# Sample-convolution products, the gated block's low part and a fill on GpSimd instead of VectorE, in layer 0's first channel mixer

## The chip, the cores and the metric

The kernel runs on one core of a Trainium2 chip. The core has five engines that run side by side, each through its own queue in program order: PE (TensorE, matmuls and transposes), DVE (VectorE), ACT (ScalarE), POOL (GpSimd) and SP (SyncE, which issues nearly all DMAs here). An instruction starts when those ahead of it on its engine are done and when the semaphores it waits for have been raised. The metric is the device time of one execution in microseconds, as the median of the runs.

## The reference

One inference step of a decoder trunk with two layers, width 1024, in fp32, for a prompt of 1024 positions and for 8 samples of 8 new positions each (64 more columns, 1088 in all). What matters here is layer 0:

```
glu = a_val * sigmoid(a_gate)                  # 512 channels
ext = concat([conv_prev, glu], axis=1)         # sample: 30 stored rows + 8 new ones
a   = causal_depthwise_conv(ext, conv_w) + b   # 31 taps for each channel
a   = silu(layer_norm(a))
b   = stick_breaking_attention(q, k, v, ...)   # samples: 8 pages of 128 keys each
h   = h + concat([a, b]) @ w_out
h   = h + (silu(g) * u) @ w_ffn_out            # g, u = split(rms_norm(h) @ w_ffn_in), 2816 each
```

For a sample the convolution of one channel is, for each of its 8 new positions, a sum over 31 products of a stored or new row with a tap.

## The kernel before, in words

Activations lie channel by channel: 128 channels on the partitions, positions along the free axis. The positions are worked on in two groups: GA, the first 512 prompt positions, and GB, the other 512 and the 64 sample columns (576). A matrix product is made in three passes from operands that are split into a high part (rounded by ACT to fp32r) and a low part (the exact value less the high part). So each weight tile `hl` costs one ACT copy (L184) and two POOL subtractions of 128x512 (L186), made up to two tiles ahead of the one in use; and each operand costs one ACT copy (L240) and one subtraction (L241), both in the helper `split`.

While PE runs the output projection and the channel mixer of GA in layer 0, the mixing work of GB is threaded in behind it. This is a background flow (`flow_c`): a Python generator that is advanced by one piece at each slot between the mixer's matmul groups. The place of a piece in every engine's queue is fixed by that at build time; nothing is scheduled at run time. The flow is, in order: the attention of GB, then the convolution of GB (`conv_b`) interleaved with the attention of the samples over their cached pages (`sample`), then the layer norm of the convolution (`conv_norm`).

The channel mixer of GA is `run_ffn` with `sig=True`; no other call has it. For each of 22 blocks f: DVE scales the gate's result out of PSUM into a buffer `tmp` (L291), ACT makes the sigmoid (L474), POOL multiplies the two (L475); DVE scales the other half (L291); at the next flush POOL multiplies both (L500, in `gated`); at the flush after that `split` makes the high part on ACT (L240) and the low part (L241) of `hid`. Two blocks later `hid` is multiplied by the second weight and DVE adds the result to the residual (L295). `tmp` has four buffers, taken in turn.

`conv_b` works on four chunks c of 128 channels. For each, DVE adds 31 taps over the 512 prompt positions into a PSUM tile `cacc` (L863, L865), two taps in a piece. After tap 11 PE transposes the stored rows (L888) and ACT copies them behind the prompt's columns in `ext` (L889). After taps 13, 15, 17 and 19 `steps` makes two sample positions each: two products of 128x248 (8 samples by 31 taps, L873) into a `tmp`, and one sum over the taps (L874).

`sample` makes, for each page group, transposes of key pages on PE (L1121), their split by ACT (L1124) and DVE (L1125, and L1132 for the new keys), scores on PE (L1144) and their gathering (L1154 on ACT, L1155 on DVE); for each of four pairs of samples it then makes the weights (L1173, L1179), fills a tile `wx` with zeros (L1181), copies the new keys' weights into it (L1184, ACT), and transposes everything (L1193) for the products with the value pages (L1216).

## Time and profile before

| what | us |
|---|---|
| median of 3 runs | 2554.57 (2547.91 to 2555.24) |
| profiled execution, device time | 2549.7 |
| its span, first to last instruction | 2547.9 |
| DVE busy in the span | 1701.0 (67%) |
| POOL busy in the span | 1566.5 (61%) |
| PE busy in the span | 2434.8 (96%) |

The span is what the trace covers; the device time of that execution is 1.8 us more. Busy times say how long an engine had an instruction running; matmuls overlap in PE's pipeline, so a busy PE is not always a PE at full rate. In the answers of the trace, a row of the windows view gives a stretch (us from the span's start), its length, then for each engine its busy time with the number of instructions, the clock granted to PE, the DMA engines' share and GB/s. A row of the timeline gives start, duration, engine, line, operation and tiles; in brackets stands the idle time of the engine before it and what ended it. A row of a group gives busy us and mean ns of one instruction behind the first bar.

### The profile page before, as it was taken

The numbers are of one execution on the slowest core, as the hardware profiler recorded it, in microseconds if no ns is written. First come the engines' busy times: TensorE is split into PE (matmuls) and PEld (weight loads), VectorE is DVE, ScalarE is ACT, GpSimd is POOL, SyncE is SP. The second block draws the span as 40 slices with busy tenths as digits, with TensorE's granted clock in tenths as the row PEclk, the third lists the DMA queues.
The fourth block names the chain that finished last, engine by engine and source line by source line (L and its number), as shares of the span: only waits on it lengthen the run. The fifth ranks groups of instructions, "written<-read, shape, count | busy, mean of one in ns | idle before, by whom it ended". The sixth has DMA issues, their size and how long they took to land.

```text
span 2547.9 us, 41426 instructions
## 1 busy us (share of the span) xinstructions
PE 2434.8 (96%) x15871; PEld 2194.1 (86%) x15871; DVE 1701.0 (67%) x2359; ACT 1104.0 (43%) x1875; POOL 1566.5 (61%) x1205
## 2 busy tenths in 40 slices
PE   8999989999999899999999999998999999999998
PEld 6789877787777678989999889888888888999997
DVE  3696877977878743766566533448776778666655
ACT  4536867753444343443433421234334334443333
POOL 6754244444443356678877622267888886887775
PEclk9999999999999999999999999999999999999999
DMA  7342241244565435223223311152333332333322
GB/s 222 115 114 74 65 118 38 75 116 122 172 178 156 136 96 159 75 67 100 86 86 94 123 42 43 49 157 59 100 92 93 98 92 84 99 96 104 100 84 79
DMA packets 355485, 258.31 MB, mean 101 GB/s; under 512 B 22913, under 2 KB 303617, under 8 KB 355272
## 3 DMA queue, kind: packets, MB, share of 16 engines
q1 hardware_dynamic: 355256, 255.66, 34.1%
q8 instruction: 126, 2.06, 0.3%
q14 instruction: 71, 0.58, 0.1%
q10 hardware_dynamic: 32, 0.01, 0.0%
HBM read 237.41 MB, written 18.69 MB: 101 GB/s over the span
## 4 chain that ended last, share of the span: by engine, by line
PE 43%; DVE 9%; POOL 3%; issue 2%; ACT 1%; POOLq 0%; DVEq 0%; ACTq 0%
PE acc L235 22%; PE acc L521 19%; DVE sum L200 2%; POOL hl L197 2%; DVE hid L241 1%; DVE hb L295 1%; DVE sum L201 1%; DVE sum L202 1%; DVE tmp L525 0%; DVE b L1677 0%; POOL tmp L500 0%; DVE sum_c L214 0%; DVE fb L1681 0%; DVE x L1677 0%; PE blk L1900 0%
## 5 line engine op out<-in xcount | busy, mean ns | idle before, releaser
L186 POOL TENSOR_TENSOR hl<-stage,hl 128x512 fp32r<-128x512 f32 x464 | 639.5, 1402 | 456.1 <-ACT hl L184 334.9
L235 PE MATMUL acc<-x,hl 128*128 128x512 f32 (+1 forms) x3648 | 781.7, 352 | 13.6 <-ACT hl L184 3.3
L235 PEld LDWEIGHTS acc<-x,hl 128*128 128x128 f32 x3648 | 587.5, 190 | 76.2 <-issue 4.9
L235 PE MATMUL acc<-hid,hl 128*128 128x288 f32 (+1 forms) x3096 | 553.7, 334 | 19.0 <-DVE hb L295 8.8
L235 PEld LDWEIGHTS acc<-hid,hl 128*128 128x128 f32 x3096 | 472.1, 190 | 74.6 <-DVE hb L295 12.6
L295 DVE TENSOR_TENSOR hb<-acc,hb 128x512 f32<-128x512 f32 (+1 forms) x360 | 255.9, 717 | 176.0 <-PE acc L235 174.7
L521 PE MATMUL acc<-x,hl 128*128 128x288 f32 (+1 forms) x2676 | 362.1, 290 | 4.7 <-POOL hl L197 1.9
L521 PEld LDWEIGHTS acc<-x,hl 128*128 128x128 f32 x2676 | 348.9, 188 | 7.0 <-POOL hl L197 2.5
L197 POOL TENSOR_TENSOR hl<-sum,hl 128x512 fp32r<-128x512 f32 x180 | 237.7, 1349 | 174.6 <-ACT hl L196 174.4
L184 ACT ACTIVATE hl<-stage 128x1024 fp32r<-128x1024 f32 x232 | 243.5, 1055 | 224.3 <-PE acc L235 140.3
L525 DVE TENSOR_TENSOR tmp<-acc,tmp 128x288 f32<-128x288 f32 (+1 forms) x420 | 173.3, 441 | 228.3 <-ACT tmp L537 135.5
L197 POOL TENSOR_TENSOR hl<-stage,hl 128x512 fp32r<-128x512 f32 x180 | 266.8, 1504 | 13.0 <-ACT hl L196 13.0
L521 PE MATMUL acc<-b,hl 128*128 128x256 f32 (+1 forms) x1548 | 216.5, 291 | 14.9 <-DVE tmp L525 11.9
L521 PEld LDWEIGHTS acc<-b,hl 128*128 128x128 f32 x1548 | 202.2, 189 | 20.4 <-ACT hl L196 13.6
L235 PE MATMUL acc<-x1t,hl 128*128 128x288 f32 x1152 | 216.3, 296 | 1.5 <-POOL hl L186 1.5
L235 PEld LDWEIGHTS acc<-x1t,hl 128*128 128x128 f32 x1152 | 195.9, 188 | 19.5 <-POOL hl L186 1.7
L196 ACT ACTIVATE hl<-sum 128x512 fp32r<-128x512 f32 x180 | 103.1, 623 | 241.3 <-DVE sum L202 219.9
L291 DVE TENSOR_TENSOR tmp<-acc,rr 128x512 f32<-128x512 f32 (+1 forms) x108 | 75.0, 708 | 106.1 <-PE acc L235 94.0
L500 POOL TENSOR_TENSOR tmp<-tmp 128x576 f32<-128x576 f32 (+1 forms) x85 | 126.3, 1486 | 16.3 <-ACT tmp L477 8.3
L196 ACT ACTIVATE hl<-stage 128x512 fp32r<-128x512 f32 x180 | 105.6, 618 | 67.7 <-PE acc L235 62.4
L241 DVE TENSOR_TENSOR hid<-tmp,hid 128x512 fp32r<-128x512 f32 (+1 forms) x88 | 99.3, 1130 | 46.0 <-ACT hid L240 45.7
L235 PE MATMUL acc<-x1a,hl 128*128 128x512 f32 x480 | 122.4, 408 | 3.0 <-POOL hl L186 1.3
(290 smaller groups left out, 3161.4 us busy)
## 6 DMA issues: line engine op xcount, KB each, us to landing
stage<-in_w_ffn_in_dram SPq DMA_DIRECT2D x176, 512.0 KB
stage<-in_w_ffn_out_dram SPq DMA_DIRECT2D x88, 512.0 KB
stage<-in_w_in_even_dram SPq DMA_DIRECT2D x40, 512.0 KB
kst<-in_cache_k_dram SPq DMA_DIRECT2D x64, 256.0 KB
vst<-in_cache_v_dram SPq DMA_DIRECT2D x64, 256.0 KB
stage<-in_w_out_even_dram SPq DMA_DIRECT2D x16, 512.0 KB
stage<-in_w_in_odd_dram SPq DMA_DIRECT2D x16, 512.0 KB
stage<-in_w_out_odd_dram SPq DMA_DIRECT2D x16, 512.0 KB
```

Of the source, the lines that this page charges most:

```text
L184: act.activation(hl[:, 0], st, AF.Copy)
L186: pool.tensor_tensor(hl[:, 1, c], st[:, c], f32(hl[:, 0, c]), op=OP.subtract)
L196: act.activation(hl[:, 0, c], x, AF.Copy)
L197: pool.tensor_tensor(hl[:, 1, c], x, f32(hl[:, 0, c]), op=OP.subtract)
L200: todo = [lambda: dve.tensor_tensor(sb, su[:, lo], su[:, hi], op=OP.add), lambda: dve.tensor_tensor(sa[:, hi], sg[:, lo], su[:, lo], op=OP ...
L235: pe.matmul(acc[:, b, :c1 - c0], w, xs[:, xi, c0 - o:c1 - o], start=first and s == 0, stop=last and s == 2)
L241: (on or dve).tensor_tensor(dst[:, 1], src, f32(dst[:, 0]), op=OP.subtract)
L291: dve.tensor_tensor(d, a, r, op=OP.mult)
L295: dve.tensor_tensor(d, a, d, op=OP.add)
L500: (dve if both and f == NF - 1 else pool).tensor_tensor(t[:, :n], t[:, :n], u[:, :n], op=OP.mult)
L521: pe.matmul(acc[:, :w2], h[:, wi, i, k], xk[:, xi], start=k == 0 and s == 0, stop=k == 3 and s == 2)
L525: dve.tensor_tensor(out, acc[:, :w2], x, op=OP.add)
```

## The change

Four edits, all in work that stands in layer 0's first channel mixer (the call with `sig=True`) or in `flow_c` behind it:

- In `gated` the low part of `hid` (L241) is made by POOL instead of DVE where `sig` is true: 22 subtractions of 128x512.
- In `steps` the products (L873) are made by POOL: 32 of 128x248.
- The sums over the taps (L874, 16 of them) stay on DVE, but each is issued after the next tap of an even number instead of right behind its products, that is in the flow's next piece.
- The zero fill of `wx` (L1181), four times, is made by POOL.

Behind the added lines the numbers move by up to two: L888 becomes L890, L1121 L1123, L1125 L1127, L1181 L1183.

```diff
             def fin():
                 (dve if both and f == NF - 1 else pool).tensor_tensor(t[:, :n], t[:, :n], u[:, :n], op=OP.mult)
-                late.append(lambda: split(dst, t[:, :n]))
+                late.append(lambda: split(dst, t[:, :n], on=pool if sig else None))
             post.append(fin)
...
                 for q in range(2):
-                    dve.tensor_tensor(p[:, q], es[:, :, q0 + q:q0 + q + CW], taps, op=OP.mult)
-                dve.tensor_reduce(new[:, q0:q0 + 2], p, axis=mybir.AxisListType.X, op=OP.add)
-
-            LATE = 6
+                    pool.tensor_tensor(p[:, q], es[:, :, q0 + q:q0 + q + CW], taps, op=OP.mult)
+                pend.append(lambda: dve.tensor_reduce(new[:, q0:q0 + 2], p, axis=mybir.AxisListType.X, op=OP.add))
+
+            LATE, pend = 6, []
...
                 tap(acc, ext[:, j:j + HALF], j)
                 if j % 2 == 0:
+                    while pend:
+                        pend.pop()()
                     continue
...
-                dve.memset(wx[bp], 0.0)
+                pool.memset(wx[bp], 0.0)
```

How the queues change, at three places. DVE, first chunk, around the third and fourth pair of sample positions (L1125 splits the transposed keys in `kth`, L291 scales a gate out of PSUM). Before:

```order
L865 SCALAR_TENSOR_TENSOR cacc<-ext,par,cacc 128x512 x2
L873 TENSOR_TENSOR tmp<-ext,par 128x248 x2
L874 TENSOR_REDUCE snew<-tmp 128x16
L865 SCALAR_TENSOR_TENSOR cacc<-ext,par,cacc 128x512 x2
L873 TENSOR_TENSOR tmp<-ext,par 128x248 x2
L874 TENSOR_REDUCE snew<-tmp 128x16
L1125 TENSOR_TENSOR kth<-m,kth 128x256 x2
L1132 TENSOR_TENSOR kth<-knew,kth 128x2x8
L241 TENSOR_TENSOR hid<-tmp,hid 128x512
L291 TENSOR_TENSOR tmp<-acc,rr 128x512
```

and after, from the second pair's sum on:

```order
L865 SCALAR_TENSOR_TENSOR cacc<-ext,par,cacc 128x512
L874 TENSOR_REDUCE snew<-tmp 128x16
L865 SCALAR_TENSOR_TENSOR cacc<-ext,par,cacc 128x512 x2
L874 TENSOR_REDUCE snew<-tmp 128x16
L865 SCALAR_TENSOR_TENSOR cacc<-ext,par,cacc 128x512
L1127 TENSOR_TENSOR kth<-m,kth 128x256 x2
L1134 TENSOR_TENSOR kth<-knew,kth 128x2x8
L291 TENSOR_TENSOR tmp<-acc,rr 128x512
L865 SCALAR_TENSOR_TENSOR cacc<-ext,par,cacc 128x512
L874 TENSOR_REDUCE snew<-tmp 128x16
```

The products and the low part of `hid` are gone from the queue, and each sum stands one tap behind where it stood.

POOL at the same chunk, all four pairs (L475 multiplies a gate by its sigmoid, L500 multiplies both halves). Before:

```order
L475 TENSOR_TENSOR tmp<-tmp 128x512
L186 TENSOR_TENSOR hl<-stage,hl 128x512 x4
L500 TENSOR_TENSOR tmp<-tmp 128x512
L475 TENSOR_TENSOR tmp<-tmp 128x512
L186 TENSOR_TENSOR hl<-stage,hl 128x512 x4
L500 TENSOR_TENSOR tmp<-tmp 128x512
```

and after:

```order
L475 TENSOR_TENSOR tmp<-tmp 128x512
L186 TENSOR_TENSOR hl<-stage,hl 128x512 x2
L873 TENSOR_TENSOR tmp<-ext,par 128x248 x2
L186 TENSOR_TENSOR hl<-stage,hl 128x512 x2
L873 TENSOR_TENSOR tmp<-ext,par 128x248 x2
L500 TENSOR_TENSOR tmp<-tmp 128x512
L475 TENSOR_TENSOR tmp<-tmp 128x512
L873 TENSOR_TENSOR tmp<-ext,par 128x248 x2
L186 TENSOR_TENSOR hl<-stage,hl 128x512 x2
L873 TENSOR_TENSOR tmp<-ext,par 128x248 x2
L241 TENSOR_TENSOR hid<-tmp,hid 128x512
L186 TENSOR_TENSOR hl<-stage,hl 128x512 x2
```

The four pairs of products stand between the weight tiles' low parts, the last behind L475, and a low part of `hid` follows them.

POOL a little later, at the first fill of `wx`. Before:

```order
L500 TENSOR_TENSOR tmp<-tmp 128x512
L475 TENSOR_TENSOR tmp<-tmp 128x512
L186 TENSOR_TENSOR hl<-stage,hl 128x512 x4
L500 TENSOR_TENSOR tmp<-tmp 128x512
L186 TENSOR_TENSOR hl<-stage,hl 128x512 x4
```

and after:

```order
L500 TENSOR_TENSOR tmp<-tmp 128x512
L475 TENSOR_TENSOR tmp<-tmp 128x512
L1183 MEMSET wx 128x128
L186 TENSOR_TENSOR hl<-stage,hl 128x512 x2
L241 TENSOR_TENSOR hid<-tmp,hid 128x512
L186 TENSOR_TENSOR hl<-stage,hl 128x512 x2
L500 TENSOR_TENSOR tmp<-tmp 128x512
```

The fill now stands behind a product that waits for ACT's sigmoid.

## The prediction, as it was made before the result was known

> **What bounds the kernel now.** I first read the page's shares of the engines, then the stage that the change touches (430 to 982 us of the span), cut at the places where the products L873 stand. The windows view (busy PE, PEld, DVE, ACT, POOL) of four stretches that hold the products of the four chunks, with their sum, and the sum of the three stretches between them:

> ```profile
> 592.00:616.00 24.00, 20.73 (x97) 16.48 (x95) 22.44 (x35) 7.33 (x15) 12.13 (x9) 0.95 0.40 111
> 671.00:692.00 21.00, 19.16 (x105) 14.86 (x103) 19.13 (x34) 8.13 (x17) 7.08 (x5) 1.00 0.64 195
> 753.00:776.00 23.00, 18.18 (x101) 13.28 (x100) 21.79 (x34) 6.66 (x15) 9.02 (x7) 0.93 0.59 174
> 836.00:858.00 22.00, 19.34 (x111) 14.84 (x104) 19.06 (x32) 7.05 (x16) 8.76 (x6) 0.95 0.58 168
> sum 90.00, PE 77.41 PEld 59.46 DVE 82.42 ACT 29.18 POOL 36.98; mean PE 19.35 PEld 14.87 DVE 20.60 ACT 7.30 POOL 9.25
> ...
> sum 176.00, PE 172.27 PEld 139.81 DVE 138.30 ACT 82.19 POOL 73.16; mean PE 57.42 PEld 46.60 DVE 46.10 ACT 27.40 POOL 24.39
> ```

> Between the product stretches PE is busy 172.27 of 176 us (97.9%) and DVE 79%. In them DVE is busy 82.42 of 90 us (92%) and PE only 77.41 (86%). PE is the engine that sets the end elsewhere; here it waits for DVE, and the granted clock is 0.93 to 0.95 in three of the four. The timeline of PE shows each wait, and that PE runs slower right after the longer ones:

> ```profile
> 577.66 3.04 PE L235 MATMUL acc<-x,hl 128*128 128x512 f32 x12
> 585.38 0.42 PE L888 MATMUL m<-ident,stc 120*128 120x120 f32 x2 [1.90 <-DVE kth L1125]
> 585.56 4.59 PE L235 MATMUL acc<-x,hl 128*128 128x512 f32 x12
> 611.09 0.77 PE L1121 MATMUL m<-ident,kst 128*128 128x128 f32 x4 [2.42 <-DVE kth L1125]
> 612.71 4.70 PE L235 MATMUL acc<-hid,hl 128*128 128x512 f32 x12 [0.84 <-DVE tmp L291]
> 689.64 0.75 PE L1144 MATMUL z<-kth,qb 128*128 128x264 f32 x4 [1.84 <-DVE zs L1155]
> 762.63 1.66 PE L235 MATMUL acc<-hid,hl 128*128 128x512 f32 x6 [1.17 <-DVE tmp L291]
> 766.40 2.34 PE L235 MATMUL acc<-hid,hl 128*128 128x512 f32 x6 [2.11 <-DVE hb L295]
> 769.42 2.08 PE L235 MATMUL acc<-hid,hl 128*128 128x512 f32 x6
> 855.94 1.11 PE L1121 MATMUL m<-ident,kst 128*128 128x128 f32 x4 [2.66 <-DVE kth L1125]
> 856.70 4.22 PE L235 MATMUL acc<-x,hl 128*128 128x512 f32 x12
> ```

> Twelve matmuls take 3.04 us at full rate, but 4.59, 4.70 and 4.22 after waits of 1.90, 2.42 and 2.66; six take 2.34 and 2.08 after 2.11, against 1.66 after a short wait. The wait of 1.84 shows no slow burst behind it. So a wait near 2 us costs itself and about 1.2 to 1.7 more. That DVE is late because of the products, its own timeline shows for the first chunk:

> ```profile
> 604.25 2.39 DVE L873 TENSOR_TENSOR tmp<-ext,par 128x248 f32<-128x248 f32 x2
> 606.67 0.67 DVE L874 TENSOR_REDUCE snew<-tmp 128x16 f32<-128x496 f32 x1
> 607.26 1.53 DVE L865 SCALAR_TENSOR_TENSOR cacc<-ext,par,cacc 128x512 f32<-128x512 f32 x2
> 608.70 1.30 DVE L873 TENSOR_TENSOR tmp<-ext,par 128x248 f32<-128x248 f32 x2
> 610.03 0.67 DVE L874 TENSOR_REDUCE snew<-tmp 128x16 f32<-128x496 f32 x1
> 610.62 0.75 DVE L1125 TENSOR_TENSOR kth<-m,kth 128x256 fp32r<-128x256 f32 x2
> ```

> DVE runs without a gap, and PE's wait at 611.09 ends with the L1125 that stands behind two pairs of products (3.7 us).

> **The change, part by part.** The rows that price it: the products on DVE in the four stretches (first sum) and the low parts L241 there (second), then groups of the trace.

> ```profile
> sum 90.00, DVE 27.42; mean DVE 6.85
> ...
> sum 90.00, DVE 2.74 POOL 0.00; mean DVE 0.68 POOL 0.00
> ...
> 585.84 0.37 ACT L889 ACTIVATE ext<-m 128x240 f32<-128x240 f32 x1 [0.72 <-PE m L888]
> 579.07 0.68 DVE L241 TENSOR_TENSOR hid<-tmp,hid 128x512 fp32r<-128x512 f32 x1
> L873 DVE TENSOR_TENSOR tmp<-ext,par x32: 584/746/1720, 592.2 to 854.3; 128x248 f32<-128x248 f32 x32
> L1125 DVE TENSOR_TENSOR kth<-m,kth 128x256 fp32r<-128x256 f32 x32 | 12.1, 415 | 8.2 <-ACT kth L1124 8.2
> L475 POOL TENSOR_TENSOR tmp<-tmp 128x512 f32<-128x512 f32 x11 | 14.7, 1338 | 52.5 <-ACT tmp L474 49.4 <-PE m L1121 3.1
> L1913 POOL TENSOR_TENSOR ss<-ss,tmp 128x320 f32<-128x320 f32 x6 | 5.2, 867 | 7.3 <-ACT tmp L1909 7.0
> L1913 POOL TENSOR_TENSOR ss<-ss,tmp 128x256 f32<-128x256 f32 x6 | 4.4, 737 | 7.1 <-ACT tmp L1909 7.0
> ```

> *Products leave DVE (the main term).* The four stretches lose 27.42 us of products and 2.74 us of L241; 52.3 us of DVE work stay. If the waits go, PE needs its 77.41 us less the slow bursts (4.70 and 4.22 against 3.04, twice six against 1.66: 1.66 + 1.18 + 1.10 = 3.9 us), so 73.5 us, at the 97.9% of the stretches between: 75.1 us instead of 90. DVE would then be at 70%, below the 79% that goes with hardly any waits. That is 14.9 us at most.

> *Products on POOL.* The trace has no POOL instruction with these operands (a broadcast, and taps that stand four columns apart). Lower bound: 737 ns for 256 columns, with (867 - 737) / 64 = 2.0 ns a column, is 0.72 us for 248. Upper bound: DVE's own longest, 1.72 us. Between them a hint: on DVE the fastest product took 584 ns where 256 columns in one row took 415, 1.41 times as long; at that ratio POOL would take 1.0 us. I take 1.0 us, P from here on.

> [...]

> *Does POOL keep up?* Of the 32 products 30 lie in the stretches. POOL's work there becomes 36.98 + 4 low parts at 1.34 (L475's mean for the same shape) + 30 P = 42.3 + 30 P: 63.9 us at the lower bound, 72.3 at P = 1.0, against 75.1 there are. So POOL fits, at 96%, but it also waits for ACT's copies in its queue, and the sums, now a piece later, wait for POOL. What helps: the first pair of a chunk needs only L889's copy (done at 586.2 us in the first chunk), so it can run before the stretch begins at 592. What hurts: a later pair stands behind L475, which waits for DVE's L291 and ACT's sigmoid. From that L291 to the pair's sum DVE has about 4 us of other work (three taps at 0.77, a sum at 0.67, a key split at 0.75 and L1155), POOL and ACT need about 2 us and 2 P. So DVE waits little at P = 1.0, and 1.4 us a chunk at P = 1.7; behind it stand L1125, L1155 and L295, for which PE waits. At 96% POOL queues will form that this does not count: I take 3 us off the main term, a fifth, 14.9 - 3 = 11.9 us.

> *Weights behind the products.* A pair of products delays the low parts L186 behind it by 2 P = 2 us. Their cover is the distance: `hl` is made two tiles ahead of the one in use, and the 24 matmuls of one tile take 6.1 us by the row above without the flow's work between. Nothing is paid unless POOL falls behind by more than that. Buffers are the other new link: in this stage 23 of DVE's L291 now wait for a POOL instruction on the same `tmp` instead of 8, but nearly all for an L475, L500 or L241 that is queued well ahead.

> *Low parts of hid on POOL, outside the stretches.* Of 22, 18 remain: about 12 us of DVE time in the rest of the stage. One matters: at 579.07 us L241 stood ahead of the L291 whose chain (sigmoid, weight copy, L1154, L1155, the key copies) ends in the 1.90 us wait at 585.38. With 0.68 us less the wait falls to about 1.2, below those that had a slow burst: 0.7 + 1.55 = 2.2 us; or nothing, if another part of the chain holds. I take 1.5. In the attention of GB ahead (430 to 560 us) five fall away from DVE, but POOL's fills of `be` queue behind them:

> ```profile
> 430.00:560.00 130.00, 124.29 (x806) 101.05 (x806) 105.79 (x104) 86.66 (x142) 64.73 (x59) 0.99 0.26 73
> 449.40 0.14 PEld L1014 LDWEIGHTS m<-ident,be 128*128 128x128 f32 x1 [2.25 <-POOL be L992]
> 446.43 1.75 DVE L241 TENSOR_TENSOR hid<-tmp,hid 128x512 fp32r<-128x512 f32 x1
> ```

> PE waits there 5.7 us in all. The wait at 449.40 is for a POOL fill behind four low parts that ran while this L241 did; without it 0 to 3 us are gained, and a low part before a fill costs 0 to 2. I take +0.5. At the stage's end the last L241 no longer stands behind L295 on DVE, but behind two L186 on POOL, and is ready earlier: +0.4.

> *The fill.* It is short on either engine; what counts is its place on POOL:

> ```profile
> 649.37 1.49 POOL L475 TENSOR_TENSOR tmp<-tmp 128x512 f32<-128x512 f32 x1 [3.12 <-PE m L1121]
> 653.38 0.60 ACT L1194 ACTIVATE wts<-m 128x512 f32<-128x512 f32 x1 [1.10 <-PE m L1193]
> ```

> At the first and third pair of samples it stands behind L475, which ended at 650.86 at the first: ACT's copies into `wx` (at 649.9 now) and the key copies behind them come some 1.2 us later, nearly covered by the 1.10 us that ACT waits soon after. Cost 0 to 1; I take 0.3.

> Sum: 11.9 + 1.5 + 0.5 + 0.4 - 0.3 = 14.0 us less. All work behind 982 us is unchanged and follows later PE by PE, so the gain reaches the end. The profiled execution took 2549.7 us (span 2547.9 and 1.8 around it): 2535.7. It lies 4.9 us below the median of the three runs, 2554.57, which gives 2540.6. I forecast **2538 us**, between the two; the rivals start from 2552, likewise.

> **Rivals.** *POOL becomes the bound, slower.* The place is the four stretches: at P = 1.6 their POOL work is 90 us, and the gain is gone; beyond that sums wait for products, L295 and L1125 wait behind the sums, and late weights follow. At P = 2.0 it is 102 us, 12 us more than now: 2564. For it speaks that no row shows POOL with such operands; against it, that P would have to exceed even DVE's longest product, 1.72, which it only took while POOL was running.

> *Nothing that can be measured.* P near 1.5 (87 us of POOL work in 90), or new waits for `tmp` and for value pages eat the gain. For pages it speaks that PE waits for them now, against it that the first of these waits (4.4 us in seven) comes at 883 us, behind the stretches:

> ```profile
> 877.30 1.09 PE L1193 MATMUL m<-ident,bet 128*128 128x128 f32 x8 [1.24 <-DVE bet L1179]
> PE o L1216 <- DMA vst<-in_cache_v_dram: 4.4, 7, 1.3
> 883.85 0.62 PE L1216 MATMUL o<-vst,wts 128*32 128x256 f32 x4 [0.59 <-DMA vst<-in_cache_v_dram]
> ```

> 2549 to 2554.

> *More than the sum.* Sums never wait (3 us), the wait at 449.40 goes with its slow burst (3 us), and the one at 877.30 (1.24 us, for the weights' L1179) too: 14 + 7 = 21 us, 2531 or below.

> **How the numbers follow.** The forecast (2532 to 2546) has 0.55, more than the sum 0.13, nothing measurable 0.22, POOL as the bound 0.10. A measurement of this kernel tells about 0.3% (7.7 us) from no change. So faster 0.68, within 0.3% 0.22, slower 0.10. The range holds the first two cases and most of the third: 2528 to 2554. The likeliest case's own range is 2532 to 2546.

> **What would show it right or wrong.** In the profile after: L873 on POOL at about 1.0 us, in four stretches that together take about 77 us instead of 90; no wait of PE above 1.5 us for DVE there, and no slow burst behind; DVE at 70 to 75%; L874 waiting under 1 us for POOL. It would be wrong if L873 takes 1.5 us or more on POOL, if PE's waits keep their places with POOL as the last releaser, or if the stage as a whole (430 to 982 us) does not become shorter by 10 us.

## The result, and the profile after

The changed kernel takes 2526.09 us (median of 7 runs, 2522.38 to 2535.0), the kernel before 2548.51 us beside it (7 runs, 2542.94 to 2555.24): a ratio of 0.992, 95% interval 0.9906 to 0.9934, or 22.4 us less. The profiled execution took 2532.55 us, 17.2 less than the profiled one of before: its stage, cut below, is 21.8 us shorter, but begins 4.3 us later, ahead of any instruction that was changed. The page's head and its shares of the engines after:

```profile
span 2530.7 us, 41450 instructions
PE 2431.9 (96%) x15871; PEld 2195.4 (87%) x15871; DVE 1659.3 (66%) x2301; ACT 1105.2 (44%) x1875; POOL 1615.9 (64%) x1263
```

DVE lost 42 us of work and POOL got 49 more, while PE's 15871 matmuls stand in the same order in both kernels. So the two traces can be cut at the same matmuls, and each piece compared. The windows view of before and then of after (busy PE, PEld, DVE, ACT, POOL; clock, DMA share, GB/s): the attention of GB, the piece up to the first products, the piece from the last products to the end of the stage; then the sum of the three pieces between the product stretches.

```profile
433.90:560.20 126.30, 120.63 (x791) 98.83 (x790) 104.39 (x97) 86.39 (x141) 64.93 (x59) 0.99 0.27 76
560.20:592.08 31.88, 29.98 (x145) 24.94 (x144) 22.60 (x37) 12.78 (x24) 12.22 (x11) 0.95 0.65 184
858.14:981.93 123.79, 115.32 (x553) 85.39 (x552) 68.43 (x93) 48.92 (x75) 71.37 (x51) 0.98 0.39 117
...
sum 176.19, PE 172.46 PEld 140.00 DVE 138.69 ACT 81.96 POOL 73.38; mean PE 57.49 PEld 46.67 DVE 46.23 ACT 27.32 POOL 24.46
```

```profile
438.22:564.91 126.69, 120.45 (x790) 98.89 (x790) 101.57 (x92) 86.62 (x141) 70.18 (x64) 0.99 0.27 75
564.91:594.99 30.08, 28.43 (x145) 23.82 (x144) 22.02 (x36) 12.79 (x24) 15.98 (x14) 1.00 0.65 192
841.96:964.44 122.48, 113.83 (x554) 84.42 (x552) 64.09 (x85) 48.49 (x75) 77.87 (x57) 1.00 0.39 119
...
sum 175.60, PE 172.23 PEld 139.64 DVE 131.06 ACT 81.10 POOL 86.44; mean PE 57.41 PEld 46.55 DVE 43.69 ACT 27.03 POOL 28.81
```

And the four product stretches, the sum before and all four after:

```profile
sum 89.87, PE 77.28 PEld 59.31 DVE 82.09 ACT 29.41 POOL 36.68; mean PE 19.32 PEld 14.83 DVE 20.52 ACT 7.35 POOL 9.17
```

```profile
594.99:613.96 18.97, 18.97 (x97) 15.99 (x95) 14.74 (x27) 8.21 (x17) 16.32 (x16) 1.00 0.40 120
668.59:687.22 18.63, 18.63 (x105) 14.88 (x103) 14.44 (x25) 8.71 (x17) 11.72 (x11) 1.00 0.68 205
747.64:763.38 15.74, 15.74 (x100) 11.99 (x99) 14.05 (x25) 6.77 (x15) 15.22 (x15) 1.00 0.79 232
823.93:841.96 18.03, 18.03 (x108) 14.25 (x101) 14.50 (x26) 7.43 (x17) 13.75 (x13) 1.00 0.65 182
sum 71.37, PE 71.37 PEld 57.10 DVE 57.72 ACT 31.12 POOL 57.01; mean PE 17.84 PEld 14.28 DVE 14.43 ACT 7.78 POOL 14.25
```

The stage from 433.90 to 981.93 us became 21.8 us shorter: the attention +0.4, the piece before the first products -1.8, the four stretches -18.5, the pieces between them -0.6, the tail -1.3. In the stretches PE is now busy without a gap (71.37 of 71.37 us) at clock 1.00. Of the 18.5 us, 12.6 were idle time of PE (89.87 - 77.28) and 5.9 were matmuls that took longer (77.28 - 71.37). About 4.2 of these 5.9 are the lower clock: the clock of the stretches before was 0.94, 1.00, 0.93 and 0.95, and the missing shares of 24.12, 22.92 and 21.99 us add up to that.

The moved work in the groups of after (minimum, median, maximum in ns; first and last start):

```profile
L873 POOL TENSOR_TENSOR tmp<-ext,par x32: 842/857/896, 590.8 to 835.5; 128x248 f32<-128x248 f32 x32
L241 POOL TENSOR_TENSOR hid<-tmp,hid x22: 1268/1296/2129, 453.3 to 951.1; 128x512 fp32r<-128x512 f32 x22
L874 DVE TENSOR_REDUCE snew<-tmp x16: 655/664/666, 597.7 to 839.5; 128x16 f32<-128x496 f32 x16
```

No sum L874 waits for POOL. A product took 0.857 us, between the prediction's lower bound of 0.72 and the 1.0 that it took for P. PE's timeline after shows what is left of the waits of which the prediction spoke:

```profile
453.38 0.33 PE L1016 MATMUL m<-ident,be 128*128 128x128 f32 x1 [1.68 <-POOL be L994]
589.84 0.42 PE L890 MATMUL m<-ident,stc 120*128 120x120 f32 x2 [1.65 <-DVE kth L1127]
590.02 3.04 PE L235 MATMUL acc<-x,hl 128*128 128x512 f32 x12
860.52 1.09 PE L1195 MATMUL m<-ident,bet 128*128 128x128 f32 x8 [1.24 <-DVE bet L1181]
```

The wait at 585.38 is 0.25 us shorter and, more important, has lost the slow burst behind it (3.04 for 4.59 us): 1.8 us together.

### The profile page after: what moved, and what is told of

Same layout as the page of the kernel before. It is cut to its first block, busy times and chain, and to the rows that moved or that the text cites. A ratio compares the mean times of both kernels' runs of the same rounds, so it can differ in the third digit from the quotient of the medians.

```text
span 2530.7 us, 41450 instructions
## 1 busy us (share of the span) xinstructions
PE 2431.9 (96%) x15871; PEld 2195.4 (87%) x15871; DVE 1659.3 (66%) x2301; ACT 1105.2 (44%) x1875; POOL 1615.9 (64%) x1263
## 4 chain that ended last, share of the span: by engine, by line
PE 43%; DVE 10%; POOL 2%; issue 2%; ACT 1%; POOLq 0%; DVEq 0%; ACTq 0%
PE acc L235 22%; PE acc L521 20%; DVE sum L200 2%; POOL hl L197 2%; DVE hb L295 1%; DVE hid L241 1%; DVE sum L201 1%; DVE sum L202 0%; DVE sum_c L214 0%; DVE b L1679 0%; DVE tmp L525 0%; POOL tmp L500 0%; DVE fb L1683 0%; PE blk L1902 0%; DVE x L1679 0%
## 5 line engine op out<-in xcount | busy, mean ns | idle before, releaser
L186 POOL TENSOR_TENSOR hl<-stage,hl 128x512 fp32r<-128x512 f32 x464 | 634.0, 1390 | 409.2 <-ACT hl L184 296.5
L235 PE MATMUL acc<-x,hl 128*128 128x512 f32 (+1 forms) x3648 | 782.8, 352 | 13.0 <-DVE tmp L291 3.0
L235 PEld LDWEIGHTS acc<-x,hl 128*128 128x128 f32 x3648 | 588.3, 190 | 74.9 <-issue 5.7
L235 PE MATMUL acc<-hid,hl 128*128 128x288 f32 (+1 forms) x3096 | 551.3, 334 | 13.0 <-DVE hb L295 5.5
L235 PEld LDWEIGHTS acc<-hid,hl 128*128 128x128 f32 x3096 | 471.3, 190 | 66.4 <-DVE hb L295 7.9
L295 DVE TENSOR_TENSOR hb<-acc,hb 128x512 f32<-128x512 f32 (+1 forms) x360 | 256.5, 719 | 178.7 <-PE acc L235 177.6
L235 PE MATMUL acc<-x1t,hl 128*128 128x288 f32 x1152 | 216.3, 295 | 1.5 <-POOL hl L186 1.5
L235 PEld LDWEIGHTS acc<-x1t,hl 128*128 128x128 f32 x1152 | 195.9, 188 | 19.5 <-POOL hl L186 1.7
L291 DVE TENSOR_TENSOR tmp<-acc,rr 128x512 f32<-128x512 f32 (+1 forms) x108 | 75.2, 711 | 139.9 <-PE acc L235 123.3
L500 POOL TENSOR_TENSOR tmp<-tmp 128x576 f32<-128x576 f32 (+1 forms) x85 | 124.7, 1468 | 9.2 <-ACT tmp L477 8.2
L235 PE MATMUL acc<-x1a,hl 128*128 128x512 f32 x480 | 122.4, 409 | 2.7 <-POOL hl L186 1.3
L252 POOL TENSOR_TENSOR ss<-ss,tmp 128x512 f32<-128x512 f32 (+1 forms) x69 | 105.1, 1523 | 29.0 <-ACT tmp L251 18.8
```

The costliest lines, as they stand in the source:

```text
L186: pool.tensor_tensor(hl[:, 1, c], st[:, c], f32(hl[:, 0, c]), op=OP.subtract)
L235: pe.matmul(acc[:, b, :c1 - c0], w, xs[:, xi, c0 - o:c1 - o], start=first and s == 0, stop=last and s == 2)
L252: pool.tensor_tensor(ss[:, g.cs], ss[:, g.cs], t[:, :g.n], op=OP.add)
L291: dve.tensor_tensor(d, a, r, op=OP.mult)
L295: dve.tensor_tensor(d, a, d, op=OP.add)
L500: (dve if both and f == NF - 1 else pool).tensor_tensor(t[:, :n], t[:, :n], u[:, :n], op=OP.mult)
```

## The experiments

In all of them the four stretches are cut at the same matmuls as above. The lengths in us, from the windows view of each run (PE's and POOL's share follow where they matter):

| kernel | chunk 1 | 2 | 3 | 4 | sum |
|---|---|---|---|---|---|
| before | 24.12 | 20.84 | 22.92 | 21.99 | 89.87 |
| after | 18.97 | 18.63 | 15.74 | 18.03 | 71.37 |
| products and later sums alone | 18.98 | 18.64 | 15.75 | 18.02 | 71.39 |
| low parts alone | 24.47 | 22.50 | 24.04 | 21.80 | 92.81 |
| half of the products | 19.00 | 18.64 | 19.22 | 18.05 | 74.91 |
| sums at once | 20.38 | 18.63 | 16.98 | 18.05 | 74.04 |
| later sums alone | 23.01 | 19.18 | 20.78 | 19.57 | 82.54 |
| products twice on POOL | 21.04 | 18.64 | 17.64 | 18.02 | 75.34 |
| products on DVE, taps in PSUM | 19.72 | 20.45 | 20.12 | 24.12 | 84.41 |
| more page buffers | 18.98 | 18.64 | 15.74 | 18.02 | 71.38 |

### Products and later sums alone

The changed kernel with the low parts and the fill given back to DVE:

```diff
-                late.append(lambda: split(dst, t[:, :n], on=pool if sig else None))
+                late.append(lambda: split(dst, t[:, :n]))
...
-                pool.memset(wx[bp], 0.0)
+                dve.memset(wx[bp], 0.0)
```

> The products on GpSimd with their sums a piece later, alone; the low parts of hid and the fill of wx stay on VectorE. My theory (VectorE was late because of the products): PE's waits in the four product stretches go as in the changed kernel, which reached the same matmuls 18.5 us earlier there; 18 to 20 us below the kernel before in all, ratio 0.992 to 0.993. Rival A (any VectorE time counts alike: the change took 27.4 us of products and 15 us of low parts off): two thirds of 22 us, so 14 to 15 us, ratio 0.994 to 0.9945.

Measured: 2527.82 us against 2545.35, ratio 0.993 (0.9913 to 0.9946), 17.5 us. The stretches are those of after to a few hundredths of a us. So the main term is this part's alone; what the other parts add can't be told apart in the time. By the traces the stage (433.90 to 981.93 us before) takes 529.6 us here against 526.2 after; of these 3.4 us, 1.8 are the piece before the first products, where the slow burst is still there.

### Low parts alone

The kernel before with one line of the change:

```diff
-                late.append(lambda: split(dst, t[:, :n]))
+                late.append(lambda: split(dst, t[:, :n], on=pool if sig else None))
```

> The low parts of hid on GpSimd, alone; products and fill stay on VectorE. My theory: one low part leaves each stretch (2.7 of 82.4 us of VectorE work), so the waits there become little shorter; with the wait at 585 us some 2 to 5 us gained, ratio 0.998 to 0.9995. Rival A (any VectorE time counts alike): one third of 22 us, 7 to 8 us, ratio 0.997. Rival B (GpSimd's fills and weight parts queue behind the low parts): slower, ratio 1.000 to 1.002.

Measured: 2544.89 us against 2545.35, ratio 0.9996 (0.9986 to 1.0005): nothing that can be told from no change. The trace shows a gain and a loss. The piece ahead of the first products loses its slow burst here too (1.8 us). But the stretches get 2.9 us longer, though 2.7 us of work left DVE there. The group of products on DVE, and PE's first long wait, in this run:

```profile
L873 DVE TENSOR_TENSOR tmp<-ext,par x32: 589/906/1735, 589.9 to 854.5; 128x248 f32<-128x248 f32 x32
```

```profile
609.79 1.09 PE L1121 MATMUL m<-ident,kst 128*128 128x128 f32 x4 [3.55 <-DVE kth L1125]
```

The median product took 906 ns instead of 746, and the wait at L1121 is 3.55 us instead of 2.42. POOL's new work made DVE's products slower: in the stretches they took 31.05 us instead of 27.34, 3.7 more, against the 2.7 that had left.

### Half of the products

As the first experiment, but of each pair one product on POOL and one on DVE:

```diff
-                    pool.tensor_tensor(p[:, q], es[:, :, q0 + q:q0 + q + CW], taps, op=OP.mult)
+                    (pool if q else dve).tensor_tensor(p[:, q], es[:, :, q0 + q:q0 + q + CW], taps, op=OP.mult)
```

> Of each two products one on GpSimd and one on VectorE, sums a piece later, nothing else changed. If what matters is whether VectorE is over some 80% busy in a stretch (79% went with hardly any waits between the stretches): half of the products leave it at about 69 of 76 us or under 90% and the waits mostly go, 13 to 18 us gained, ratio 0.993 to 0.995. If the gain goes with the time taken off: half of what the products bring, 8 to 10 us, ratio 0.996 to 0.997.

Measured: 2528.89 us, ratio 0.9936 (0.9919 to 0.9954), 16.5 us. Three stretches are as short as with all products moved; only the third is not, and its row shows why:

```profile
740.52:759.74 19.22, 17.25 (x101) 12.72 (x99) 18.28 (x31) 6.66 (x15) 11.43 (x10) 0.94 0.76 225
...
757.15 4.60 PE L235 MATMUL acc<-hid,hl 128*128 128x512 f32 x12 [1.97 <-DVE hb L295]
```

One wait of 1.97 us with its slow burst (4.60 for 3.04) makes up the 3.5 us. The sums come later here too, and that alone brings 7.3 us in the stretches (below). On top of it half of the products bring 7.6 us, where all of them bring 11.2. So the gain is not in proportion to the work taken off DVE; it is complete in a stretch once PE's waits there are gone, since PE then has no gap left.

### Sums at once

The changed kernel with each sum right behind its products:

```diff
-                pend.append(lambda: dve.tensor_reduce(new[:, q0:q0 + 2], p, axis=mybir.AxisListType.X, op=OP.add))
+                dve.tensor_reduce(new[:, q0:q0 + 2], p, axis=mybir.AxisListType.X, op=OP.add)
```

> The changed kernel, but each sum issued right behind its products instead of in the next piece. If the delay of the sums is needed to cover GpSimd's 2 x 0.857 us, VectorE waits for GpSimd at up to 16 sums, 1 to 3 us each where the products stand behind weight parts or a product that waits for the sigmoid: 10 to 20 us of VectorE waits, and 3 to 10 us of the gain lost, ratio 0.994 to 0.997. If the products run ahead of VectorE anyway, since they wait for nothing that it makes: as the changed kernel, ratio 0.992.

Measured: 2528.43 us, ratio 0.9936 (0.9919 to 0.9953), 16.9 us. DVE now does wait for POOL, 12.3 us in six waits, of which this is one:

```profile
602.38 0.67 DVE L874 TENSOR_REDUCE snew<-tmp 128x16 f32<-128x496 f32 x1 [2.01 <-POOL tmp L873]
```

It costs only 2.7 us of the stretches (74.04 against 71.37), because DVE has slack there once the products are gone (in the stretches of after it is busy for 57.72 of 71.37 us). So the delay of the sums adds little to the moved products; whether it does in the time is within the intervals.

### Later sums alone

The kernel before with the products on DVE and only the sums a piece later:

```diff
-                dve.tensor_reduce(new[:, q0:q0 + 2], p, axis=mybir.AxisListType.X, op=OP.add)
+                pend.append(lambda: dve.tensor_reduce(new[:, q0:q0 + 2], p, axis=mybir.AxisListType.X, op=OP.add))
...
                 if j % 2 == 0:
+                    while pend:
+                        pend.pop()()
                     continue
```

> The kernel before with one part of the change alone: the products stay on DVE, only each sum L874 comes a piece of the flow later. Theory (the stretches are set by how much time DVE's work takes there, and the delay only covers a wait that the move to POOL makes): no measurable effect, ratio to the kernel before 0.998 to 1.002, DVE's busy time in the stretches near the 82 us of before. Rival (DVE lost time between a product and its sum, or the order of sums and key copies alone set PE's waits): 3 to 8 us faster, with shorter waits of PE for L1127 at the same products.

My theory fell here. Measured: 2535.76 us against 2547.23, ratio 0.9953 (0.9939 to 0.9966), 11.5 us, and 7.3 us in the stretches by the traces. The sum of the stretches, and two waits of PE in this run:

```profile
sum 82.54, PE 75.28 PEld 57.98 DVE 75.99 ACT 28.97 POOL 36.65; mean PE 18.82 PEld 14.49 DVE 19.00 ACT 7.24 POOL 9.16
```

```profile
610.61 0.77 PE L1123 MATMUL m<-ident,kst 128*128 128x128 f32 x4 [1.46 <-DVE kth L1127]
763.17 2.42 PE L235 MATMUL acc<-hid,hl 128*128 128x512 f32 x6 [1.84 <-DVE hb L295]
```

DVE is busy for the same share of the stretches as before (75.99 of 82.54 us, 92%; before 82.09 of 89.87, 91%). No instruction left its queue; what PE waits for only stands one sum further ahead in it. The wait at L1123 fell from 2.42 to 1.46 us and no slow burst follows it; only the one of 1.84 still has one (six matmuls in 2.42). So it is not DVE's share that sets the stretches but what stands ahead of L1127, L291 and L295. Of the 7.3 us, 5.3 are idle time of PE (12.6 before, 7.3 here) and 2.0 are its slower matmuls, since fewer of the shorter waits have a slow burst behind them. A sum of 0.67 us less ahead of each wait is a part of the 5.3; the products also took 0.8 us less in the stretches (26.56 us for 27.34); the traces do not split the rest. Nor do they account for the other 4 us of the medians' difference: the stage as a whole is 7.5 us shorter, and the profiled execution took 2540.04 us, 4.3 above the median of this run. Executions differ by such amounts ahead of the change too (below).

### Products twice on POOL

The changed kernel, each product made twice, with the same result:

```diff
-                for q in range(2):
+                for q in (0, 1, 0, 1):
                     pool.tensor_tensor(p[:, q], es[:, :, q0 + q:q0 + q + CW], taps, op=OP.mult)
```

> The changed kernel with every product made twice on POOL, one after the other with the same result (64 instead of 32): this doubles the price P of a pair for POOL and leaves all else. The prediction's count (POOL's work in the stretches 42.3 + 30 P us, P now 2 x 0.857 = 1.71) gives 93.7 us in stretches that now take 71.4: the gain of 18.5 us there would be gone, time 2544 to 2553, POOL the last releaser of DVE's L874 and of PE's weights. Theory from the traces (10 of the 32 products already start ahead of the stretches, and POOL is busy 86 of 176 us between them, so products can run early; the sums wait where they can't): DVE waits for POOL in the first stretch most, 6 to 12 us of the 18.5 stay, time 2532 to 2540.

Measured: 2537.79 us against 2547.23, ratio 0.9961 (0.9948 to 0.9973), 9.4 us. The sum of the stretches:

```profile
sum 75.34, PE 72.19 PEld 57.01 DVE 54.68 ACT 29.55 POOL 71.42; mean PE 18.05 PEld 14.25 DVE 13.67 ACT 7.39 POOL 17.86
```

POOL is busy for 95% of the stretches and yet 14.5 of the 18.5 us stay, since products run ahead of the stretches. The rest of the loss comes behind them, and not where I looked for it. POOL's, DVE's and PE's timelines around the end of the fourth stretch:

```profile
832.87 6.54 POOL L873 TENSOR_TENSOR tmp<-ext,par 128x248 f32<-128x248 f32 x8
839.36 2.54 POOL L186 TENSOR_TENSOR hl<-stage,hl 128x512 fp32r<-128x512 f32 x2
841.86 1.27 POOL L500 TENSOR_TENSOR tmp<-tmp 128x512 f32<-128x512 f32 x1
...
838.09 5.06 DVE L1134 TENSOR_TENSOR kth<-knew,kth 128x16 fp32r<-128x16 f32 x1
...
845.44 0.74 PE L1146 MATMUL z<-kth,qb 128*128 128x264 f32 x4 [3.01 <-DVE zs L1157]
```

A subtraction of 128x16 with a median of 0.17 us before (L1132 there) took 5.06 on DVE: it ended at 843.15, when POOL's run of instructions without a gap ended (843.13). PE then waited 3.01 us for what stood behind it on DVE. This wait and the slower matmuls right behind it are 4.8 of the 8.3 us by which the tail (130.75 us) is longer than after. Sums wait for POOL too, 9.9 us in six waits. So POOL as the bound reaches PE through DVE's own instructions, not only through late sums.

### Products on DVE, taps in PSUM

The kernel before; the 124 taps are copied once by ACT to the free half of the PSUM bank of `o`, and the products read them there:

```diff
-            taps = par[:, CONVW + c:CONVW + 4 * CW:4][:, None, :].to_broadcast([128, 8, CW])
+            taps = box_tp["t"][:, c:4 * CW:4][:, None, :].to_broadcast([128, 8, CW])
...
+            big = op_.tile([128, 512], F, name="o")
+            box_tp["t"] = big[:, 256:380]
+            act.activation(box_tp["t"], par[:, CONVW:CONVW + 124], AF.Copy)
```

> The kernel before, with the 124 taps copied once to a free half of a PSUM bank (one ACT copy) and read from there by the products, which stay on DVE, sums right behind them. Nothing is taken off DVE. Theory (in the kernel before, L873 is the one large instruction of DVE with both inputs in SBUF, and it takes 0.57 to 0.6 us where POOL is idle and 1.1 to 1.75 where POOL runs, while L291 and L865 beside the same POOL work keep their 0.68 and 0.75 us; so some 11 of the 28 us of products in the stretches were spent waiting for POOL and not working): L873 takes near 0.6 us throughout, DVE's work in the stretches falls from 82 to about 71 us, and 9 to 14 us of the time go: 2534 to 2540, half and more of the change's gain with no work moved. Rival (the slow products have another cause, such as their operands' form, or POOL's work is slowed instead): L873 keeps its mean of 0.97 us, and the time stays within 0.2%.

Measured: 2541.23 us against 2547.23, ratio 0.9975 (0.9963 to 0.9987), 6.0 us. The group of products, and PE's timeline:

```profile
L873 DVE TENSOR_TENSOR tmp<-ext,o x32: 403/405/408, 591.5 to 842.5; 128x248 f32<-128x248 f32 x32
```

```profile
675.57 1.07 PE L1219 MATMUL o<-vst,wts 128*32 128x256 f32 x16 [1.77 <-DVE tmp L873]
842.97 1.93 PE L1219 MATMUL o<-vst,wts 128*32 128x256 f32 x16 [3.49 <-DVE tmp L873]
```

All 32 products take 403 to 408 ns, where before they took 584 to 1720 beside the same work of POOL. (Before, the 14 that began while POOL was idle took 584 to 617 ns, and 17 of the 18 others 746 to 1720; each of these 17 ended 456 to 486 ns after the end of a POOL instruction that was running when it began.) So their long durations were time spent waiting for POOL, as the theory said. Even an undisturbed product is 0.18 us shorter with its taps in PSUM. That is not the price of a second input in SBUF as such: L241, which has both there, takes 0.68 us for 512 columns when undisturbed, the same as L291 with one of them in PSUM. It belongs to the taps, which stand four columns apart and are broadcast; which of the two costs it was not tried. (So L873 is not the only large instruction of DVE with both inputs in SBUF, as the expectation had it; L241 is another.) In the stretches the products fall from 27.34 to 10.85 us. The time did not fall as far as the theory said (5.5 us in the stretches instead of 9 to 14), because the edit made a new wait: the taps share the tile `o` with the products of the value pages, and PE's L1219 (L1216 of the kernel before) now waits for L873 four times, 7.8 us in all. Whether the stretches would have come to 71.4 us without it was not tried.

### More page buffers, and one more low part on POOL

The changed kernel, aimed at what is left in the stage:

```diff
-                dve.tensor_tensor(qz[hh][r], qs, f32(q[r]), op=OP.subtract)
+                pool.tensor_tensor(qz[hh][r], qs, f32(q[r]), op=OP.subtract)
...
-            KP = 6
+            KP = 4
...
-                    vst[i] = sa.tile([128, 2, 512], F, name="vst", bufs=2)
+                    vst[i] = sa.tile([128, 2, 512], F, name="vst", bufs=3)
...
-                load_v(i + 3)
+                load_v(i + 4)
```

> The changed kernel, and two things more: three buffers for the value pages instead of two (two key buffers fewer make room), and the low part of the query tile in the attention ahead (L969) on POOL instead of DVE. It aims at what is left in the stage after the change: PE's waits for value pages (about 5 us at 867 to 881 us) and for DVE's L1006 (about 5 us at 453 to 515). Theory (what is left is single waits that a transfer or DVE sets): 3 to 8 us less than the changed kernel, 2518 to 2523. Rival (the pages come as fast as the queues bring them, and POOL's fills of the weights are late behind its new work): the waits move, within 2 us of the changed kernel or slower.

Measured: 2533.42 us against 2547.23, ratio 0.994 (0.992 to 0.9959): no better than the changed kernel, by intervals that overlap. The waits moved, as the rival said: PE's last wait for a page here, and one of those for DVE in the attention, are

```profile
880.67 1.36 PE L1218 MATMUL o<-vst,wts 128*32 128x256 f32 x6 [2.30 <-DMA vst<-in_cache_v_dram]
492.70 0.96 PE L1016 MATMUL m<-ident,be 128*128 128x128 f32 x7 [2.18 <-DVE be L1006]
```

against at most 1.40 and 2.05 us after. In sum PE waits 4.9 us for pages (5.6 after) but 8.1 us for L1006 (4.5 after). No version tried here beats the changed kernel.

## Why the prediction was right and wrong

The direction and the place were right: faster, in the four stretches, by PE's waits for DVE. The time was not: 2538 us forecast, 2526.09 measured, 1.9 us below the low end of the range, 2528. Of the 12 us, 3.5 are the starting level (2552 taken, 2548.51 measured beside the changed kernel) and 8.4 are the gain (14.0 forecast, 22.4 measured). Counted from the level measured beside it, the range would have been 2524.5 to 2550.5 and holds the time. Step by step:

**Products leave DVE: 11.9 us forecast, 18.5 measured.** This is the term that was mis-sized, in three places. (1) *PE's own need.* I took PE's 77.41 us less 3.9 for slow bursts, counting only the four groups of L235 that I had compared; the whole excess over PE's time without waits was 5.9 us (77.28 against 71.37), 2.0 more. (2) *The 97.9%.* I gave the stretches the share of PE that the pieces between them had, 75.1 us; they went to 100%, 1.6 us more. (3) *The 3 us for sums that wait for POOL.* No sum waits. I counted 30 products in stretches of 75 us at 1.0 us, 96% for POOL; measured are 57.01 of 71.37 us, 80%, because a product took 0.857 us and because ten of the 32 start ahead of the stretches, so that 18.7 us of products fell into them and not 30; POOL's other work there was 38.3 us where I had 42.3. With sums at once the allowance of 3 us would have been right (2.7). 2.0 + 1.6 + 3 is the 6.6 us that was missing.

**The picture behind it was partly wrong.** I expected DVE at 70% of the stretches, and took 79% as the share that goes with hardly any waits. DVE is at 81% (57.72 of 71.37) and PE has no gap; with later sums alone DVE stayed at 92% and 7.3 us went. What counts is what stands ahead of the few instructions for which PE waits, and whether a slow burst follows the wait that results. The sums' delay, which I only took as a cover for waits on POOL, shortens those waits by itself. The two parts don't add up (7.3 us for the delay alone, 15.8 for the change without it, 18.5 together), since PE can't do better than no gap.

**The wait at 585.38: 1.5 us forecast, 1.8 measured,** of which 0.25 is the wait and 1.55 the slow burst. The piece before the first products is 1.8 us shorter with the low parts alone as well. In all five traces with the low parts on POOL the wait is 1.65 us and no burst follows; in the five without them it is 1.90 to 1.96, and four have the burst, but that with half of the products (1.96) has none. So the 0.25 us is the low part's; that the burst went is helped by it and partly luck. The prediction took the length of a wait as what decides; it is not the length alone (last section).

**The attention: +0.5 forecast, -0.4 measured.** PE's wait for POOL's L994 (L992 before) fell from 2.01 to 1.68 us only, and its slow burst is still there (six matmuls in 2.54 us; 2.74 before); the 2.25 us of the prediction's row are those of the weight load, which became 1.91. The waits for L1006 grew from 3.5 to 4.5 us in all. **The stage's end: 0.4 forecast, 1.3 measured** over the whole tail. **The fill:** its cost of 0.3 us can't be seen in the pieces between the stretches, which became 0.6 us shorter.

**Low parts in the stretches** I counted as 2.74 us of relief. Alone they are a loss of 2.9 us there, because the products on DVE took longer beside POOL's subtractions (31.05 us in the stretches for 27.34). Together with the moved products that loss has no object, and nothing of it is seen. The prediction had the row that says so (a product took up to 1.72 us, "which it only took while POOL was running") and used it only as an upper bound for P.

**The rivals.** *More than the sum* (0.13, 2531 or below) is where the time fell, with one of its three legs: the sums never wait; the waits at 449.40 and 877.30 that it let go are still there (1.68 and 1.24 us after). *POOL becomes the bound* was put too near: at 1.71 us for a product's price, where I had the gain gone, 9.4 us are left. The count of 30 P in the stretches failed there; 40.97 of some 55 us of products fell into them. *Nothing measurable* is excluded by the interval.

Of what was to show it: the product near 1.0 us (0.857), no wait above 1.5 us and no slow burst in the stretches (none at all), L874 waiting under 1 us (not at all), the stage shorter by 10 us or more (21.8) came true; the stretches' 77 us (71.4) and DVE's 70 to 75% (81%) did not.

## What to carry to other kernels

Price a relief of an engine by the wait it shortens: list what stands between the waited-for instruction and its inputs, take the removed time off that wait, and add the slow clock behind it where there is one (here 1.55 us behind the wait at 585.38); the cap is then all idle time of PE in the stretch and all its excess over full rate (here 12.6 and 5.9 us), and it may be reached by a part of the change. An instruction on DVE whose duration varies by a factor of two or three beside a busy POOL, as L873 did here (584 to 1720 ns), may be waiting and not slow. More work on POOL made it worse here (a median of 906 ns for 746); moving it to POOL took away its work and its waiting on DVE together, and moving one of its inputs out of SBUF the waiting (403 to 408 ns).

## What the runs showed of the hardware that was not expected

**DVE did not always get its turn between two POOL instructions.** In the run with products made twice the 128x16 subtraction took 5.06 us, through the rest of a series of products, two subtractions of 1.27 us and a product of 1.27 us. So it stayed blocked over several of POOL's instructions in a row. It is one case: the other 15 subtractions of that run took at most 1.40 us, and before, at 441 to 449 us, four subtractions of POOL took 8.05 us in a row while L965, L1004 and L241 on DVE took 1.75 to 1.76 each, as if the two engines took turns. What makes the difference the runs do not show.

```profile
586.61 0.42 PE L890 MATMUL m<-ident,stc 120*128 120x120 f32 x2 [1.95 <-DVE kth L1127]
586.80 4.59 PE L235 MATMUL acc<-x,hl 128*128 128x512 f32 x12
```

```profile
580.90 0.42 PE L890 MATMUL m<-ident,stc 120*128 120x120 f32 x2 [1.96 <-DVE kth L1127]
581.09 3.04 PE L235 MATMUL acc<-x,hl 128*128 128x512 f32 x12
```

```profile
426.71 3.12 PE L235 MATMUL acc<-x,hl 128*128 128x512 f32 x11 [2.60 <-DVE x L382]
```

```profile
427.20 5.06 PE L235 MATMUL acc<-x,hl 128*128 128x512 f32 x11 [2.60 <-DVE x L382]
```

What differs is to be seen in the granted clock. In all ten traces it is halved for 3.41 us at a time or for a whole multiple of that (but for one at the very end of each): before 12 times for 3.41 us; after seven times for 3.41, once for 6.83 and once for 10.24. In one execution all these times begin on one grid of 3.41 us, which lies differently in each execution. The first pair, cut on its grid (length, PE's busy time, clock):

```profile
583.70:587.11 3.41, 1.46 (x11) 1.00 0.38 87
587.11:590.52 3.41, 3.41 (x10) 0.50 0.73 211
```

```profile
576.42:579.84 3.42, 2.53 (x15) 1.00 0.05 10
579.84:583.25 3.41, 2.35 (x11) 1.00 0.70 225
583.25:586.66 3.41, 3.41 (x21) 1.00 0.67 189
```

In the first the whole wait of 1.95 us falls into one piece of the grid, and the next piece runs at half clock; in the second the 1.96 us are parted, 0.89 and 1.06. The 2.60 us of the second pair are parted too: PE is idle 1.68 and 0.95 us of two pieces before, and 2.00 and 0.60 after, where the slow time, 10.24 us or three pieces, comes behind the 2.00. Counted over the ten traces, outside halved pieces: of 7132 pieces in which PE was idle for less than 1.59 us none was followed by a halved one, of 71 with 1.59 to 1.95 us 38 were, and all 57 with 1.95 us or more (in before and after alone, from the first record of the clock on, 20 us into the span: none of 1420, 8 of 12, all 15). So in the first pair a wait of about 2 us cost 1.55 us more (4.59 for 3.04) where it fell into one piece, and nothing where it was parted so that no piece had 1.59 us of idle time; in the second the three slow pieces cost 1.94 us in the burst shown (5.06 for 3.12). That is one source of the few us by which executions of one kernel differ, and in the last pair it sits ahead of the change.
